# Layer 0 of a two-layer trunk: input and output projections as seven half-size products for eight, output projection behind all of y, norm first, Silu gate

## The chip, the core and the metric

The kernel runs on one core of a Trainium2 chip. The metric is the device time of one execution in microseconds (us), as the median of several runs. The engines are TensorE (PE, matmuls into PSUM), VectorE (DVE), ScalarE (ACT), GpSimd (POOL) and SyncE (SP, which here only issues DMAs). Each works through its own instructions in the order in which they stand in the program, and they wait for each other on semaphores.

## What is computed

Two layers on 1024 tokens of width 1024 in float32. Layer 0 is a pooling mixer, layer 1 stick-breaking attention; only layer 0 and the step into layer 1 matter here.

```python
D_MODEL, SEQ, D_INNER = 1024, 1024, 2048
POOL_WINDOWS = (2, 4, 8, 16)           # 4 groups of 512 channels

def causal_pool_minus_self(u, window): # trailing mean over min(t+1, window) positions, minus u[t]
    ...

def pooling_mixer(u, w_in, w_group, scale, w_out):
    proj = u @ w_in                    # (1024 x 1024) @ (1024 x 4096)
    xb, z = jnp.split(proj, 2, axis=-1)
    xg = xb.reshape(B, S, N_POOL_GROUPS, POOL_GROUP_DIM)
    pooled = jnp.stack(
        [causal_pool_minus_self(xg[:, :, gi], w) for gi, w in enumerate(POOL_WINDOWS)],
        axis=2)
    mixed = jnp.einsum('bsgi,gio->bsgo', pooled, w_group).reshape(B, S, D_INNER)
    y = mixed * scale * jax.nn.silu(z)
    return y @ w_out                   # (1024 x 2048) @ (2048 x 1024)

def reference(x, ...):
    h = x
    for i in range(DEPTH):             # layer 0: pooling_mixer, layer 1: attention
        u = rms_norm(h, norm_g[i])
        h = h + mixer(u)
    return rms_norm(h, norm_f)
```

## The kernel before

A float32 product is carried by three passes (`mm3`, L76 to L79): each operand is split into hi and lo parts, and hi·hi, hi·lo and lo·hi are accumulated in PSUM. A weight tile of 128x512 is split by an ACT copy (L91) and a DVE subtraction (L92). Nearly all matmuls of layer 0 have 128 rows and 512 columns. Tokens run in reversed order on the chip.

Layer 0 works on channels by rows and tokens by columns. x comes transposed from HBM (`xt`). The input is multiplied by the norm's gain (L162 on ACT, L163 on DVE for the remainder) but not by the norm's factor of a token: that factor, `rsb` on all partitions, is made beside the first products from a second copy of x (`load_h`, L99 to L103, L175, L176) and comes in on DVE when a projection leaves PSUM (`scaled`, L179). So the first matmul needs only one tile of x and one of weights.

A loop over the four windows then does, in each: four blocks of 128 channels of xb (`xb_block`: two halves of 512 tokens, each 8 contraction blocks times 3 passes, so 48 matmuls; doubling additions L204, a ratio L206, the subtraction L207, a split L209/L210); four blocks of gate (`gate`, 48 matmuls each, scaled, Sigmoid, product); and behind each gate block the group matrix on the pooled data (`mixed`, 24 matmuls, L223, and the split of y). Behind every second block the output projection of the two finished 128-row blocks of y is done at once (`late`, `out_proj`, L139 adds it onto h): 96 matmuls each time. The last of these are interleaved with the norm of layer 1 (`normed`) and 64 transposes of 128x128 (`transposed`, L114, L117, L118). In all, layer 0 has 1536 matmuls of input projection, 384 of group matrices and 768 of output projection.

The order on each engine is set by a scheduler that simulates the program; the loops above are the order in which it is written. POOL does little: memsets, the norm's small steps (L101, L103), and in layer 1 the masks (memset L433, selects L438 and L448, each 128x128), while DVE does scans with two SBUF inputs (L441).

Of the kernel before, what the change touches and what calls it, by code (L numbers as in the profile page):

```python
# [9 lines left out]
F32 = mybir.dt.float32  # L10
# [5 lines left out]
P = 128  # L16
# [3 lines left out]
NT = S // P          # token tiles  # L20
NK = D // P          # contraction blocks of the model width
# [15 lines left out]
def trunk(ctx, tc, x, xt, g, pw, pg, psc, pwo, sqk, sv, sz, swo, nf, out):  # L37
# [16 lines left out]
    ul = resid.tile([P, NK, S], F32R, name="ul")

# [4 lines left out]
    act(warm, warm, AF.Sigmoid)  # L60
# [4 lines left out]
    nc.gpsimd.memset(mhalf, -0.5)  # L65

    # Ratio of the full window to the window that the sequence start cuts off.
# [8 lines left out]
    def mm3(ps, lh, ll, rh, rl, start, stop):  # L76
        nc.tensor.matmul(ps, lhsT=lh, rhs=rh, start=start, stop=False)  # L77
        nc.tensor.matmul(ps, lhsT=lh, rhs=rl, start=False, stop=False)  # L78
        nc.tensor.matmul(ps, lhsT=ll, rhs=rh, start=False, stop=stop)  # L79

    def load_w(*srcs):
        """Load [128, n] blocks of weights and split them into (hi, lo) tiles of 512 columns."""
        tiles = []
        for src in srcs:
            n = src.shape[-1]
            raw = wraw.tile([P, D], F32, name="w_raw")
            nc.sync.dma_start(raw[:, :n], src)
            for c in range(0, n, 512):
                wh = wspl.tile([P, 512], F32R, name="w_hi")
                wl = wspl.tile([P, 512], F32R, name="w_lo")  # L90
                act(wh, raw[:, c:c + 512], AF.Copy)  # L91
                nc.vector.tensor_tensor(wl, raw[:, c:c + 512], wh, ALU.subtract)  # L92
                tiles.append((wh, wl))
        return tiles

    def rstd_of(t):
        ssq = small.tile([P, 1], F32, name="ssq")
        junk = small.tile([P, D], mybir.dt.bfloat16, name="junk", bufs=1)
        act(junk, h[:, t, :], AF.Square, accum_out=ssq)  # L99
        ms = small.tile([P, 1], F32, name="ms")  # L100
        nc.gpsimd.tensor_scalar(ms, ssq, 1.0 / D, EPS, ALU.mult, ALU.add)  # L101
# [4 lines left out]
    def normed(t, xt):  # L106
        rs = rstd_of(t)
        nc.vector.tensor_scalar_mul(xt, h[:, t, :], rs)

    def transposed(layer, half, xn):  # L110
        for k in range(NK):
            tp = ps_t.tile([P, 512], F32, name="pt")
            for j in range(4):
                nc.tensor.transpose(tp[:, j * P:(j + 1) * P], xn[j][:, k * P:(k + 1) * P], ident)  # L114
            gc = g_sb[:, layer * NK + k:layer * NK + k + 1]
            cs = slice(half * 512, half * 512 + 512)
            act(uh[:, k, cs], tp, AF.Copy, scale=gc)  # L117
            nc.vector.scalar_tensor_tensor(  # L118
                ul[:, k, cs], in0=tp, scalar=gc, in1=uh[:, k, cs], op0=ALU.mult, op1=ALU.subtract)

    def proj_ch(w2, half, pool=None):
        """[128 channels, 512 tokens] of u @ w for one block of 128 columns."""
        ps = pool.tile([P, 512], F32, name="pq") if pool else ps_d.tile([P, 512], F32, name="pd")
        cs = slice(half * 512, half * 512 + 512)
        for k in range(NK):
            wh, wl = w2[k // 4]
            ks = slice(k % 4 * P, k % 4 * P + P)
            mm3(ps, wh[:, ks], wl[:, ks], uh[:, k, cs], ul[:, k, cs], k == 0, k == NK - 1)
        return ps

    def out_proj(ys, w4, t):
        """h[t] += sum over two blocks of 128 rows; ys: (hi, lo) of [128, 128] each."""
        for n in range(2):
            po = ps_d.tile([P, 512], F32, name="pd")
            for i, (yh, yl) in enumerate(ys):
                wh, wl = w4[2 * i + n]
                mm3(po, yh, yl, wh, wl, i == 0, i == 1)
            cs = slice(n * 512, n * 512 + 512)
            nc.vector.tensor_tensor(h[:, t, cs], po, h[:, t, cs], ALU.add)  # L139

# [1 line left out]
    with tc.tile_pool(name="l0", bufs=2) as l0:  # L142
        def xn_tile(t):
            return l0.tile([P, S + 16], F32, name="xb" if t % 2 else "wsum")[:, :D]
# [3 lines left out]
        rsb = l0.tile([P, S], F32, name="rsb", bufs=1)  # L148
        xv = x.rearrange("(t p) c -> t p c", p=P)

        xs = {}

        def load_ut(half, ks, then=None):
            cs = slice(half * 512, half * 512 + 512)
            for k in ks:
                if k % 2 == 0:
                    xs["t"] = xn_tile(k // 2)
                xj = xs["t"][:, k % 2 * 512:k % 2 * 512 + 512]
                nc.sync.dma_start(xj, xt[k * P:(k + 1) * P, cs])
                if then:  # L160
                    then(k)
                act(uh[:, k, cs], xj, AF.Copy, scale=g_sb[:, k:k + 1])  # L162
                nc.vector.scalar_tensor_tensor(  # L163
                    ul[:, k, cs], in0=xj, scalar=g_sb[:, k:k + 1], in1=uh[:, k, cs],
                    op0=ALU.mult, op1=ALU.subtract)

        def load_h(half):
            for t in range(4 * half, 4 * half + 4):
                nc.sync.dma_start(h[:, t, :], xv[t])

        def factors(half):
            ps = ps_t.tile([P, 512], F32, name="pt")
            for j in range(4):
                rs = rstd_of(4 * half + j)
                nc.tensor.transpose(ps[:, j * P:(j + 1) * P], rs.broadcast_to([P, P]), ident)  # L175
            act(rsb[:, half * 512:half * 512 + 512], ps, AF.Copy)  # L176

        def scaled(dst, ps, half):
            nc.vector.tensor_tensor(dst, ps, rsb[:, half * 512:half * 512 + 512], ALU.mult)  # L179

        def gate(w2, half, t):
            ps = proj_ch(w2, half)
            scaled(t, ps, half)
            act(ps, t, AF.Sigmoid)
            nc.vector.tensor_tensor(t, ps, t, ALU.mult)

        def xb_block(gi, c, w2, pooled):
            w = WINDOWS[gi]
            xb = l0.tile([P, S + 16], F32, name="xb")
            nc.gpsimd.memset(xb[:, S:], 0.0)  # L190
            if gi == 0:
                pss = first[c]
            else:
                pss = [proj_ch(w2, half) for half in range(2)]
            if len(pss) < 2:
                pss.append(proj_ch(w_first[c], 1))
            for half in range(2):
                scaled(xb[:, half * 512:half * 512 + 512], pss[half], half)
# [12 lines left out]

        def mixed(gi, o, pooled, t0):
            kb = gi * 4 + o
            (gh, gl), = load_w(pg[kb])
            yh = l0.tile([P, S], F32R, name="y_h", bufs=4)
            yl = l0.tile([P, S], F32R, name="y_l", bufs=4)
            for half in range(2):
# [424 lines left out]
```

## Time and profile before

| | |
|---|---|
| median of 3 runs | 1613.57 us (1613.32 to 1613.58) |
| span of the profiled execution | 1613.1 us |
| PE busy | 99% |
| DVE / ACT / POOL busy | 65% / 37% / 10% |
| layer 0 ends, layer 1 begins | at about 640 us |

The profile gives each engine's busy time and, for groups of instructions, their count and mean duration. Matmuls are pipelined: one of 128x512 is listed with some 390 ns but the next begins after 0.23 us, so their pace is read from the count in a window and not from the mean. DVE instructions overlap a little too: "x2 | 1.30" is two instructions that begin one behind the other. A timeline's bracket gives the idle time before an instruction and what ended it.

### The profile page before, as it was taken

The numbers are of one execution on the slowest core, as the hardware profiler recorded it, in microseconds if no ns is written. First come the engines' busy times: TensorE is split into PE (matmuls) and PEld (weight loads), VectorE is DVE, ScalarE is ACT, GpSimd is POOL, SyncE is SP. The second block draws the span as 40 slices with busy tenths as digits, with TensorE's granted clock in tenths as the row PEclk, the third lists the DMA queues.
The fourth block names the chain that finished last, engine by engine and source line by source line (L and its number), as shares of the span: only waits on it lengthen the run. The fifth ranks groups of instructions, "written<-read, shape, count | busy, mean of one in ns | idle before, by whom it ended". The sixth has DMA issues, their size and how long they took to land.

```text
span 1613.1 us, 22462 instructions
## 1 busy us (share of the span) xinstructions
PE 1592.7 (99%) x8520; PEld 1365.5 (85%) x8520; DVE 1050.7 (65%) x1601; ACT 594.3 (37%) x1140; POOL 161.5 (10%) x673
## 2 busy tenths in 40 slices
PE   7999999999999999999999999999999999999997
PEld 6888888888888887888988988989989989989986
DVE  4745665565567557387767757757757757757678
ACT  6212121112112314355435335435335335435344
POOL 1000000000000001011101101102102102101112
PEclk9999999999999999999999999999999999999999
DMA  7102111111102110121021021021021021021012
GB/s 281 59 27 66 46 53 46 40 52 46 59 27 66 46 55 31 40 66 40 27 66 40 27 66 40 27 66 40 27 66 40 27 66 41 27 66 40 27 52 106
DMA packets 30139, 85.87 MB, mean 53 GB/s; under 512 B 4048, under 2 KB 4048, under 8 KB 30032
## 3 DMA queue, kind: packets, MB, share of 16 engines
q1 hardware_dynamic: 29888, 84.43, 16.4%
q8 instruction: 67, 1.10, 0.3%
q14 instruction: 40, 0.33, 0.1%
q10 hardware_dynamic: 144, 0.01, 0.0%
HBM read 71.84 MB, written 4.19 MB: 47 GB/s over the span
## 4 chain that ended last, share of the span: by engine, by line
PE 96%; DVE 2%; DMA 1%; ACT 0%; issue 0%; POOL 0%; SPq 0%; DVEq 0%; POOLq 0%; ACTq 0%
PE pd L77 27%; PE pd L78 27%; PE pd L79 27%; PE pt L473 4%; PE po L77 2%; PE po L79 2%; PE po L78 2%; PE pq L429 2%; PE pq L430 2%; DMA w_raw<-in_pw 0%; DVE h L139 0%; DVE om L441 0%; PE pt L114 0%; PE pq L77 0%; PE pq L79 0%; PE pq L78 0%
## 5 line engine op out<-in xcount | busy, mean ns | idle before, releaser
L77 PE MATMUL pd<-uh,w_hi 128*128 128x512 f32 x992 | 389.5, 393 | 0.7 <-DVE t L340 0.7
L78 PE MATMUL pd<-ul,w_hi 128*128 128x512 f32 x992 | 390.0, 393 | 0.1
L79 PE MATMUL pd<-uh,w_lo 128*128 128x512 f32 x992 | 385.8, 391 | 0.0
L91 ACT ACTIVATE w_hi<-w_raw 128x512 fp32r<-128x512 f32 x236 | 148.6, 631 | 368.1 <-PE pd L78 203.3
L441 DVE TENSOR_TENSOR_SCAN om<-om 128x257 f32<-128x257 f32 (+1 forms) x192 | 187.8, 979 | 84.6 <-POOL om L438 67.0
L92 DVE TENSOR_TENSOR w_lo<-w_raw,w_hi 128x512 fp32r<-128x512 f32 x236 | 161.6, 690 | 98.4 <-ACT w_hi L91 96.1
L77 PEld LDWEIGHTS pd<-uh,w_hi 128*128 128x128 f32 x992 | 186.8, 188 | 38.4 <-DVE t L340 1.1
L79 PEld LDWEIGHTS pd<-uh,w_lo 128*128 128x128 f32 x992 | 186.6, 188 | 38.1
L78 PEld LDWEIGHTS pd<-ul,w_hi 128*128 128x128 f32 x992 | 186.8, 188 | 37.7 <-DVE ul L118 0.9
L139 DVE TENSOR_TENSOR h<-pd,h 128x512 f32<-128x512 f32 x256 | 172.7, 686 | 64.0 <-PE pd L79 62.7
L77 PE MATMUL pd<-w_hi,y_h 128*128 128x512 f32 x512 | 205.5, 401 | 0.7 <-ACT y_h L502 0.4
L78 PE MATMUL pd<-w_lo,y_h 128*128 128x512 f32 x512 | 202.5, 395 | 0.0
L79 PE MATMUL pd<-w_hi,y_l 128*128 128x512 f32 x512 | 200.7, 394 | 0.0
L434 ACT ACTIVATE om<-pq 128x256 f32<-128x256 f32 (+1 forms) x192 | 94.4, 492 | 178.4 <-PE pq L430 171.0
L77 PE MATMUL pd<-w_hi,uh 128*128 128x256 f32 x512 | 146.6, 286 | 0.0
L78 PE MATMUL pd<-w_lo,uh 128*128 128x256 f32 x512 | 144.8, 283 | 0.0
L79 PE MATMUL pd<-w_hi,ul 128*128 128x256 f32 x512 | 144.7, 283 | 0.0
L79 PEld LDWEIGHTS pd<-w_hi,y_l 128*128 128x128 f32 x512 | 96.3, 188 | 21.3 <-DVE y_l L503 0.2
L477 DVE TENSOR_TENSOR at_l<-pt,at_h 128x512 fp32r<-128x512 f32 (+1 forms) x160 | 99.3, 627 | 21.9 <-ACT at_h L476 21.6
L77 PEld LDWEIGHTS pd<-w_hi,y_h 128*128 128x128 f32 x512 | 96.4, 188 | 20.0 <-DVE h L139 0.8
L78 PEld LDWEIGHTS pd<-w_lo,y_h 128*128 128x128 f32 x512 | 96.5, 189 | 18.8
L445 DVE TENSOR_TENSOR om<-pq,om 128x256 f32<-128x256 f32 (+1 forms) x192 | 105.4, 551 | 8.4
(99 smaller groups left out, 2393.1 us busy)
## 6 DMA issues: line engine op xcount, KB each, us to landing
w_raw<-in_pw SPq DMA_DIRECT2D x30, 512.0 KB, 3.3
w_raw<-in_pwo SPq DMA_DIRECT2D x16, 512.0 KB, 3.3
w_raw<-in_sqk SPq DMA_DIRECT2D x16, 512.0 KB, 3.3
w_raw<-in_sz SPq DMA_DIRECT2D x16, 512.0 KB, 3.3
w_raw<-in_sv SPq DMA_DIRECT2D x16, 512.0 KB, 3.3
w_raw<-in_swo SPq DMA_DIRECT2D x16, 512.0 KB, 3.3
h<-in_x SPq DMA_DIRECT2D x8, 512.0 KB, 6.9
w_raw<-in_pg SPq DMA_DIRECT2D x16, 256.0 KB, 2.7
```

The lines of the kernel that those rows point to most:

```text
L77: nc.tensor.matmul(ps, lhsT=lh, rhs=rh, start=start, stop=False)
L78: nc.tensor.matmul(ps, lhsT=lh, rhs=rl, start=False, stop=False)
L79: nc.tensor.matmul(ps, lhsT=ll, rhs=rh, start=False, stop=stop)
L91: act(wh, raw[:, c:c + 512], AF.Copy)
L92: nc.vector.tensor_tensor(wl, raw[:, c:c + 512], wh, ALU.subtract)
L139: nc.vector.tensor_tensor(h[:, t, cs], po, h[:, t, cs], ALU.add)
L429: nc.tensor.matmul(ps[:, :m], lhsT=ql, rhs=kh[:, k1 - m:k1], start=True, stop=False)
L434: act(om[:, 1:1 + n], pz, AF.Sigmoid, scale=-ZSCALE)
L441: nc.vector.tensor_tensor_scan(out=om[:, :1 + n], data0=om[:, :1 + n], data1=om[:, :1 + n], initial=1.0 if s.first else carry[r], op0=ALU. ...
L445: nc.vector.tensor_tensor(om[:, :n], pz, om[:, :n], ALU.mult)
L473: nc.tensor.transpose(tp[:, c * P:(c + 1) * P], om[:, (j - b0) * P:(j - b0 + 1) * P], ident)
L477: nc.vector.tensor_tensor(al[:, :n], tp[:, :n], ah[:, :n], ALU.subtract)
```

## The change

**Input projection.** The contraction (two halves of 512) and the tokens (two halves of 512) and pairs of 128-channel blocks make a 2x2 by 2x2 product, done with seven half-size products (Strassen, in Winograd's form). A pair of blocks costs 7 x 12 = 84 matmuls where it cost 96. The operands of x are seven sets of four tiles (`G[1]` to `G[7]`), made once: `to_u` (L173) scales a tile by gain and token factor, `u_sums` makes the sums, two of its four on DVE (L186, L189) and two on POOL (L188, L192), and `u_split` splits each. The sums of weights are made for every pair on POOL (L232, L233, L234, L257). The products' outputs are combined on DVE (`v`, `x_`, `out`) into xb or, with Silu on ACT, into the gate `t0`.

**Norm first.** Since x's sums need finished u, the column sums of squares come first: ACT squares the loaded tiles (L154), PE sums them with a matmul against ones (L156), then DVE, POOL, four transposes and an ACT copy make `rsb` (L160 to L167).

**Output projection behind all of y.** `mixed` stores each y block to HBM (`y_dram`, L297). After the last window the whole projection is done as seven products of 96 matmuls, in the order 1, 6, 2, 7, 4, 5, 3: y is loaded again in halves (L356), sums of y and of weights are made on POOL (40 additions for product 6: L404, L405, L406, L410, L411; 8 each for products 7, 4 and 3: L430, L434, L470; 8 onto h: L477, L483), and all of them are split as before. The norm of layer 1 and its transposes stand half between products 5 and 3 and half behind 3 (`to_u1`).

Layer 1 has the same work; its weight tiles are loaded in 512 columns at a time, and h is kept as 16 separate tiles.

```diff
-        load_ut(0, (0,), load_first)
-        load_ut(0, (1, 2, 3))
...
-        first = [[proj_ch(w_first[c], 0, ps_q if c < 2 else None)] for c in range(4)]
-        load_h(0)
-        factors(0)
-        load_ut(1, range(8))
...
+        def to_u(k, l, n, rsb):
+            j, kb = divmod(k, 4)
+            t = B[j, l, kb]
             nc.vector.scalar_tensor_tensor(
+                t, in0=t, scalar=g_sb[:, k:k + 1], in1=rsb, op0=ALU.mult, op1=ALU.mult)
+            if n:
+                u_split(n, kb, t)
...
+        def u_sums(kb):
+            b11, b21, b12, b22 = B[0, 0, kb], B[1, 0, kb], B[0, 1, kb], B[1, 1, kb]
+            t3 = l0.tile([P, 512], F32, name="w_raw", bufs=3)
+            nc.vector.tensor_tensor(t3, b22, b12, ALU.subtract)
+            u_split(7, kb, t3)
+            nc.gpsimd.tensor_tensor(b12, b11, b12, ALU.subtract)
+            nc.vector.tensor_tensor(b11, t3, b11, ALU.add)
+            u_split(6, kb, b11)
+            u_split(5, kb, b12)
+            nc.gpsimd.tensor_tensor(b11, b11, b21, ALU.subtract)
+            u_split(4, kb, b11)
...
+                add = nc.gpsimd.tensor_tensor
+                add(s1, a21, a22, ALU.add)
+                add(a21, a21, a11, ALU.add)
+                add(a11, a11, s1, ALU.add)
...
+        x0, x1 = Group(0), Group(2)
+        rsb = load_x(0, {1: x0.load, 3: x1.load})
+        for k in range(4):
+            to_u(k, 0, 1, rsb)
+        x0.first()
+        x1.first()
+        for k in range(4, 8):
+            to_u(k, 0, 2, rsb)
+        x0.second()
+        x1.second()
+        rsb = load_x(1)
+        for kb in range(4):
+            to_u(kb, 1, 0, rsb)
+            to_u(4 + kb, 1, 3, rsb)
+            u_sums(kb)
...
+            nc.sync.dma_start(y_dram[kb], t0)
...
+        def ops6(kb):
+            for jl in ((0, 1), (1, 1), (1, 0)):
+                load_y(*jl, kb)
+            T3[kb] = slot()
+            add(T3[kb], Y[1, 1, kb], Y[0, 1, kb], ALU.subtract)
+            add(Y[0, 1, kb], Y[0, 0, kb], Y[0, 1, kb], ALU.subtract)
+            add(Y[0, 0, kb], T3[kb], Y[0, 0, kb], ALU.add)
+            a21, a22, a11 = (wload(*ij, kb) for ij in ((1, 0), (1, 1), (0, 0)))
+            S1[kb] = ob.tile([P, 512], F32, name="s1", bufs=8)
+            S2[kb] = ob.tile([P, 512], F32, name="s2", bufs=8)
+            add(S1[kb], a21, a22, ALU.add)
+            add(S2[kb], S1[kb], a11, ALU.add)
+            return split(S2[kb]), split(Y[0, 0, kb], ob, "y")
```

Where the order moves. First PE at the start of the program. Before, `uh`/`ul` are the parts of x and `y_h`/`y_l` the parts of the first weights:

```order
L77 MATMUL pq_198<-uh_83,y_h_132 128x512
L78 MATMUL pq_198<-ul_84,y_h_132 128x512
L77 MATMUL pq_223<-uh_83,y_h_134 128x512
L78 MATMUL pq_223<-ul_84,y_h_134 128x512
L79 MATMUL pq_198<-uh_83,y_l_133 128x512
```

After, behind eight groups of column sums; `wsum`/`xb` hold squares, `rs4` the norm's factors, `g1` the first operand of x:

```order
L156 MATMUL bk_121<-ones_79,xb_184 128x2 x4
L165 MATMUL bk_194<-ident_72,rs4_192 128x128 x4
L88 MATMUL bk_221<-g1_0h_202,w_hi_222 128x512
L88 MATMUL bk_240<-g1_0h_202,w_hi_241 128x512
L156 MATMUL bk_315<-ones_79,wsum_318 128x2 x4
...
L156 MATMUL bk_315<-ones_79,wsum_366 128x2 x3
L156 MATMUL bk_315<-ones_79,xb_374 128x2 x4
L165 MATMUL bk_384<-ident_72,rs4_382 128x128 x4
L88 MATMUL bk_512<-g6_0h_405,w_hi_515 128x512
L89 MATMUL bk_512<-g6_0l_406,w_hi_515 128x512
```

The first products now stand behind the factors of one token half, and the sixth product (`g6`), after 48 matmuls, behind those of the other half.

POOL at the same place. Before, its rows of layer 0 are the norm's small steps and memsets:

```order
L190 MEMSET xb_430 128x16
L190 MEMSET xb_440 128x16
L101 TENSOR_SCALAR ms_398<-ssq_395 128x1
L103 TENSOR_TENSOR rs_400<-ms_398,mhalf_96 128x1
L101 TENSOR_SCALAR ms_406<-ssq_403 128x1
```

After, `pl` are tiles of u and `a_raw` loaded weights:

```order
L162 TENSOR_TENSOR rs4_382<-ms4_380,mhalf_77 128x4
L188 TENSOR_TENSOR pl_316<-pl_122,pl_316 128x512
L188 TENSOR_TENSOR pl_324<-pl_130,pl_324 128x512
L188 TENSOR_TENSOR pl_332<-pl_140,pl_332 128x512
L232 TENSOR_TENSOR w_raw_508<-a_raw_504,a_raw_506 128x512
L233 TENSOR_TENSOR a_raw_504<-a_raw_504,a_raw_132 128x512
L234 TENSOR_TENSOR a_raw_132<-a_raw_132,w_raw_508 128x512
L188 TENSOR_TENSOR pl_340<-pl_148,pl_340 128x512
L192 TENSOR_TENSOR pl_122<-pl_122,pl_158 128x512
```

Thirteen 128x512 additions now stand between the second factors and the last operand of the fourth product.

POOL where the output projection begins, after the last window; `slot` are halves of y, `w_raw` output weights, `s1` and `s2` their sums. Before, nothing stands there but the small steps of layer 1's norm:

```order
L190 MEMSET xb_3546 128x16
L101 TENSOR_SCALAR ms_4227<-ssq_4224 128x1
L103 TENSOR_TENSOR rs_4229<-ms_4227,mhalf_96 128x1
L101 TENSOR_SCALAR ms_4252<-ssq_4249 128x1
L103 TENSOR_TENSOR rs_4254<-ms_4252,mhalf_96 128x1
```

After:

```order
L404 TENSOR_TENSOR slot_3739<-slot_3735,slot_3733 128x512
L405 TENSOR_TENSOR slot_3733<-slot_3529,slot_3733 128x512
L410 TENSOR_TENSOR s1_3749<-w_raw_3743,w_raw_3745 128x512
L406 TENSOR_TENSOR slot_3529<-slot_3739,slot_3529 128x512
L411 TENSOR_TENSOR s2_3750<-s1_3749,w_raw_3747 128x512
L410 TENSOR_TENSOR s1_3789<-w_raw_3783,w_raw_3785 128x512
L404 TENSOR_TENSOR slot_3779<-slot_3775,slot_3773 128x512
L434 TENSOR_TENSOR slot_3529<-slot_3529,slot_3737 128x512
```

The row that writes the last `slot` operand of the sixth product is the 45th of such rows, five of them (L434) for the fourth product.

SP at that place, first before (output weights inside the windows), then after (`t0` is y of a block, stored ahead of the loads that follow):

```order
L87 DMA w_raw_4147<-in_pg 128x512
L87 DMA w_raw_4187<-in_pwo 128x1024
L87 DMA w_raw_4197<-in_pwo 128x1024
L87 DMA w_raw_4523<-in_sqk 128x1024
L87 DMA w_raw_4601<-in_sz 128x1024
```

```order
L297 DMA y_dram_114<-t0_3325 128x1024
L297 DMA y_dram_114<-t0_3326 128x1024
L356 DMA slot_3529<-y_dram_114 128x512
L103 DMA w_raw_3531<-in_pwo 128x512
L356 DMA slot_3553<-y_dram_114 128x512
L103 DMA w_raw_3555<-in_pwo 128x512
```

The loads of the first output product are issued only when the last block of y has been stored.

## Rows read from the trace of the kernel before

**Rows 1.** The page, parts 1 and 4: busy time by engine, chain of waits by engine

```profile
PE 1592.7 (99%) x8520; PEld 1365.5 (85%) x8520; DVE 1050.7 (65%) x1601; ACT 594.3 (37%) x1140; POOL 161.5 (10%) x673
PE 96%; DVE 2%; DMA 1%; ACT 0%; issue 0%; POOL 0%; SPq 0%; DVEq 0%; POOLq 0%; ACTq 0%
```

**Rows 2.** Windows of layer 0: window, length, then busy us and instructions by engine

```profile
200.00:400.00 200.00, 200.00 (x875) 163.99 (x874) 119.20 (x162) 43.53 (x67) 0.67 (x6) 1.00 0.15 49
400.00:600.00 200.00, 200.00 (x873) 163.73 (x872) 117.70 (x162) 39.52 (x61) 0.22 (x2) 1.00 0.15 49
```

**Rows 3.** Groups on POOL: form and count, busy us, mean ns, idle before

```profile
L448 POOL TENSOR_SCALAR_AFFINE_SELECT om<-om 128x128 f32<-128x128 f32 x128 | 55.2, 432 | 118.2 <-DVE om L445 118.1
...
L433 POOL MEMSET om<- 128x1 f32 x192 | 18.2, 98 | 305.2 <-DVE om L441 119.8 <-PE pt L473 87.6 <-DVE h L139 61.2
...
masks.py:199 POOL TENSOR_SCALAR_AFFINE_SELECT ident<-ident 128x128 f32<-128x128 f32 x1 | 0.3, 292 | 0.0
```

**Rows 4.** Timeline of POOL in layer 1: start us, duration us, instruction

```profile
993.48 0.29 POOL L438 TENSOR_SCALAR_AFFINE_SELECT om<-om 128x128 f32<-128x128 f32 x1 [1.11 <-ACT om L434]
...
995.05 0.82 POOL L448 TENSOR_SCALAR_AFFINE_SELECT om<-om 128x128 f32<-128x128 f32 x1 [0.84 <-DVE om L445]
...
997.56 0.62 POOL L448 TENSOR_SCALAR_AFFINE_SELECT om<-om 128x128 f32<-128x128 f32 x1 [1.54 <-DVE om L445]
```

**Rows 5.** Timeline of DVE over the same stretch

```profile
993.54 0.77 DVE L92 TENSOR_TENSOR w_lo<-w_raw,w_hi 128x512 fp32r<-128x512 f32 x1
...
994.84 0.94 DVE L441 TENSOR_TENSOR_SCAN om<-om 128x385 f32<-128x385 f32 x1
...
997.35 0.68 DVE L92 TENSOR_TENSOR w_lo<-w_raw,w_hi 128x512 fp32r<-128x512 f32 x1
```

**Rows 6.** Timeline of PE: first matmuls, and the first on pooled data

```profile
10.34 1.05 PE L77 MATMUL pq<-uh,y_h 128*128 128x512 f32 x2
11.20 0.48 PE L78 MATMUL pq<-ul,y_h 128*128 128x512 f32 x1
...
67.06 0.40 PE L77 MATMUL pd<-pooled,w_hi 128*128 128x512 f32 x1
```

**Rows 7.** DMA view of 0 to 30 us: GB/s moved, in 40 slices

```profile
GB/s 0 0 71 323 169 127 156 229 320 331 328 366 404 402 407 407 404 380 404 399 421 415 399 426 391 399 415 396 382 382 388 391 388 384 375 380 410 421 399 404
```

**Rows 8.** Timeline of ACT at the start

```profile
15.11 1.16 ACT L91 ACTIVATE w_hi<-w_raw 128x512 fp32r<-128x512 f32 x2 [0.55 <-DMA w_raw<-in_pw]
```

**Rows 9.** Timeline of DVE at the start

```profile
9.21 0.75 DVE L163 SCALAR_TENSOR_TENSOR ul<-wsum,g_sb,uh 128x512 fp32r<-128x512 f32 x1
9.88 1.42 DVE L163 SCALAR_TENSOR_TENSOR ul<-xb,g_sb,uh 128x512 fp32r<-128x512 f32 x2
...
15.77 1.30 DVE L92 TENSOR_TENSOR w_lo<-w_raw,w_hi 128x512 fp32r<-128x512 f32 x2 [0.43 <-ACT w_hi L91]
...
35.67 0.69 DVE L92 TENSOR_TENSOR w_lo<-w_raw,w_hi 128x512 fp32r<-128x512 f32 x1 [2.91 <-ACT w_hi L91]
```

**Rows 10.** Groups on DVE in 60 to 640 us, columns as in Rows 3

```profile
L223 DVE SCALAR_TENSOR_TENSOR t<-pd,sc_sb,t 128x512 f32<-128x512 f32 x32 | 23.9, 750 | 22.4 <-PE pd L79 22.4
...
L207 DVE SCALAR_TENSOR_TENSOR wsum<-wsum,xb 128x1024 f32<-128x1024 f32 x13 | 15.9, 1221 | 0.2
```

**Rows 11.** The page, part 6: loads of 256 KB, us from issue to landing

```profile
w_raw<-in_pg SPq DMA_DIRECT2D x16, 256.0 KB, 2.7
```

**Rows 12.** Windows at the end of layer 0, all instructions, then the transposes L114 alone

```profile
600.00:660.00 60.00, 57.17 (x265) 44.39 (x264) 37.90 (x56) 27.83 (x47) 6.83 (x24) 0.97 0.12 38
640.00:648.00 8.00, 6.91 (x25) 5.22 (x25) 3.29 (x5) 1.37 (x2) 0.00 (x0) 0.79 0.01 2
...
600.00:660.00 60.00, 10.71 (x64) 7.88 (x64) 0.97 0.12 38
```

More of the change, by code (lines that the diff above doesn't have):

```diff
@@ L59, in trunk @@
     nc.vector.memset(warm, 0.0)
-    act(warm, warm, AF.Sigmoid)
+    act(warm, warm, AF.Silu)
     sc_sb = const.tile([P, DI // P], F32, name="sc_sb")
@@ L73, in trunk @@
         ratio[w] = r
[L76 to L94, printed above, removed]
@@ new lines, in split, with raw_of, rstd_of @@
+    def split(raw, pool=None, name="w"):
+        pool = pool or wspl
+        hi = pool.tile([P, 512], F32R, name=f"{name}_hi")
+        lo = pool.tile([P, 512], F32R, name=f"{name}_lo")
+        act(hi, raw, AF.Copy)
+        nc.vector.tensor_tensor(lo, raw, hi, ALU.subtract)
+        return hi, lo
+    def raw_of(src, pool, name="w_raw", **kw):
+        raw = pool.tile([P, 512], F32, name=name, **kw)
+        nc.sync.dma_start(raw, src)
+        return raw
+    def rstd_of(parts):
+        n = len(parts)
+        ssq = small.tile([P, 2], F32, name="ssq")
+        for i, part in enumerate(parts):
+            junk = small.tile([P, 512], mybir.dt.bfloat16, name="junk", bufs=1)
+            act(junk, part, AF.Square, accum_out=ssq[:, i:i + 1])
+        if n == 2:
+            nc.gpsimd.tensor_tensor(ssq[:, 0:1], ssq[:, 0:1], ssq[:, 1:2], ALU.add)
@@ L121, in proj_ch @@
[L121 to L139, printed above, removed]
@@ L142, in trunk @@
[L142 to L187, printed above, removed]
-            w = WINDOWS[gi]
[L189 to L198, printed above, removed]
@@ L208, in xb_block @@
                 cur[:, :S], in0=cur[:, :S], scalar=1.0 / w, in1=xb[:, :S], op0=ALU.mult, op1=ALU.subtract)
-            act(pooled[0][:, c, :], cur[:, :S], AF.Copy)
-            nc.vector.tensor_tensor(pooled[1][:, c, :], cur[:, :S], pooled[0][:, c, :], ALU.subtract)
+            for half in range(2):
+                cs = slice(half * 512, half * 512 + 512)
+                hi, lo = pooled[c, half] = pl_tile(F32R), pl_tile(F32R)
+                act(hi, cur[:, cs], AF.Copy)
+                nc.vector.tensor_tensor(lo, cur[:, cs], hi, ALU.subtract)
@@ L257, in trunk @@
+        x0, x1 = Group(0), Group(2)
[9 more added lines that the diff above has]
+        rsb = load_x(1)
+        for kb in range(4):
+            to_u(kb, 1, 0, rsb)
+            to_u(4 + kb, 1, 3, rsb)
+            u_sums(kb)
         nc.sync.dma_start(sc_sb, psc)
-        load_h(1)
-        factors(1)
@@ L285, in trunk @@
-        w4 = load_w(pwo[14], pwo[15])
-        for half in (1, 0):
-            xn = []
-            for t in range(4 * half, 4 * half + 4):
-                out_proj(y_of(ys[-2:], t), w4, t)
-                xn.append(xn_tile(t))
-                normed(t, xn[-1])
-            transposed(1, half, xn)
-    with tc.tile_pool(name="l1", bufs=1) as l1:
+            pooled = {}
+            for cp in (0, 2):
+                grp = (x0 if cp == 0 else x1) if gi == 0 else Group(gi * 4 + cp)
+                if gi:
+                    grp.first()
+                dst = [xb_tile() for _ in range(2)]
+                grp.rest(dst, AF.Copy)
+                for i in range(2):
+                    pool_block(gi, cp + i, dst[i], pooled)
@@ new lines, in trunk, with slot @@
+            for op in (0, 2):
+                grp = Group(16 + gi * 4 + op)
+                grp.first()
+                dst = [l0.tile([P, S], F32, name="t0") for _ in range(2)]
+                grp.rest(dst, AF.Silu)
+                for i in range(2):
+                    mixed(gi, op + i, pooled, dst[i])
+    slots_ = ctx.enter_context(tc.tile_pool(name="slots", bufs=48, reuse_waits="tile"))
+    def slot(dtype=F32):
+        return slots_.tile([P, 512], dtype, name="slot")
+    h, u = {}, {}
@@ new lines, in trunk, with out_proj @@
+    ps_ctx.close()
+    act(warm, warm, AF.Sigmoid)
+    ps_d = ctx.enter_context(tc.tile_pool(name="ps_d", bufs=3, space=PSUM, reuse_waits="tile"))
+    ps_q = ctx.enter_context(tc.tile_pool(name="ps_q", bufs=2, space=PSUM, reuse_waits="tile"))
+    ps_t = ctx.enter_context(tc.tile_pool(name="ps_t", bufs=2, space=PSUM, reuse_waits="tile"))
+    ps_o = ctx.enter_context(tc.tile_pool(name="ps_o", bufs=1, space=PSUM, reuse_waits="tile"))
+    def out_proj(ys, w4, t):
+        for n in range(2):
+            po = ps_d.tile([P, 512], F32, name="pd")
+            for i, (yh, yl) in enumerate(ys):
+                wh, wl = w4[2 * i + n]
+                mm3(po, yh, yl, wh, wl, i == 0, i == 1)
+            nc.vector.tensor_tensor(h[t, n], po, h[t, n], ALU.add)
@@ L296, in trunk, with load_w @@
+    with tc.tile_pool(name="l1", bufs=1, reuse_waits="tile") as l1:
+        def load_w(*srcs):
+            return [split(raw_of(src[:, c:c + 512], l1, bufs=4))
+                    for src in srcs for c in range(0, src.shape[-1], 512)]
         NPAIR = NH // 2
@@ L391, in finish @@
             if not nfb:
[L392 to L394 removed]
+                for n in range(2):
+                    b = l1.tile([P, 512], F32, name="w_raw", bufs=4)
+                    nc.sync.dma_start(b, nf[:, n * 512:n * 512 + 512].broadcast_to([P, 512]))
+                    nfb.append(b)
             if t < LATE_T and not ended:
```

313 lines of the change are left out of this document (226 added, 87 removed).

## The prediction

> **What bounds the kernel now.** First the busy shares and the chain of waits [rows 1]: TensorE (PE) is busy 99% of the span and carries 96% of the chain, VectorE (DVE) 65%, GpSimd (POOL) 10%. What the reader is to see: nothing but PE time is on the path, so removed matmuls pay in full only while every operand is still ready in time. Then PE's pace in undisturbed layer 0 [rows 2]: 400 us hold 875 + 873 matmuls, 0.2289 us each. Then the start, the end of layer 0, and the engine that the change loads most, POOL.
>
> **Products removed: −65.9 us.** Before, layer 0 has 1536 matmuls of input projection, 384 with the group matrices and 768 of output projection. After, seven products for eight: 1344 + 384 + 672 = 2400. The 288 removed are worth 288 × 0.2289 = 65.9 us. The order of the changed kernel has these counts, so the change does what it says there; the question is what feeds them.
>
> **The price of one POOL addition, a.** The change puts on POOL 128x512 float32 additions of two SBUF tiles: 8 in the u sums, 4 for each of 16 groups, 64 for the output products and 8 for h. No row of before shows one, so I bound it. POOL's 128x128 select takes 292 ns undisturbed and its smallest memset 98 ns [rows 3]: (292 − 98)/128 = 1.52 ns an element for one read. One such pass over 512 columns is 0.87 us, the low end; were each operand a pass, 98 + 2 × 776 = 1.65, the high end. Counting two reads and a write against one read and a write gives 1.26. I take **a = 1.2**, near that middle and a little under it, because the select also compares. The Trainium skill, GPSIMD Engine Reference, section 3.1, has a 2048-element float32 add at 4497 ns, which by length would be an estimated 1.12 us here; with the sum below that is 1635. No run here shows it.
>
> **Does POOL stand still beside DVE?** The same select has a mean of 432 ns where it waits its turn late in the kernel [rows 3]. The timelines show why [rows 4, 5]: it takes 0.29 alone, but 0.82 from 995.05, when a DVE scan with two SBUF inputs runs from 994.84 to 995.78, and 0.62 from 997.56, beside the split L92 that ends at 998.03. Both times POOL ends 0.1 to 0.15 after DVE. The other way, the L92 at 993.54 takes 0.77 where the one at 997.35 takes 0.68: POOL had begun at 993.48. So I count a POOL addition and a DVE operation with two SBUF inputs as exclusive, save about 0.2 us (POOL's 98 ns fixed part and the 0.08 by which DVE's successive operations overlap). The Trainium skill, same page, section 1, says that POOL shares its SBUF interfaces with such DVE instructions; the trace agrees with its 0.82 and 0.62 for 0.29. Its section 4.1 speaks against the change: an elementwise add of two inputs belongs on VectorE.
>
> **Start: +44.5 us.** Before, the first matmul on pooled data is at 67.06 with five blocks of 48 in front of it [rows 6], so 67.06 − 240 × 0.229 = 12.1 us are lost. Norm first makes the operands of the first product wait for all column sums. Loads run at 400 GB/s [rows 7], 0.65 us for 256 KB, and ScalarE (ACT) starts on the 14th such unit at 15.1, two copies in 1.16 [rows 8]. In the new order ACT writes the first factors only behind the squares of the 16th load: 15.1 + 1.3 + 0.6 for a square (as a copy) + 0.6 for the copy = 17.6. DVE then scales eight tiles at 0.67 (1.42 for two, less 0.75 for one) = 5.4, and the first remainder, 0.61 (1.30 less 0.69), is there at 23.6 [rows 9]. 48 matmuls follow, 11.0 us, with some 12 at the 0.43 that the first ones of before show (11.20 − 10.34 for two) [rows 6], +2.4: 37.0. Behind them stand the last column sums, the power, four transposes and a copy: 2.4, so the second factors are ready at 39.4. Now DVE has 41 operations up to the last remainder of the fourth product: 8 × 0.67 + 33 × 0.61 = 25.5. Interlocked with them are 13 POOL additions, at 13 × (a − 0.2) = 13.0 if exclusive. That is 78, where PE has done 93 matmuls = 21.3. Lost: 56.6, so +44.5 against before; 31.5 without exclusion.
>
> **Middle of layer 0: +3, from 0 to 10.** Per window PE has 432 matmuls = 98.9 us. DVE has 60 operations at 0.61, 8 at 0.67 and four pooling blocks of two to five passes of 1.22 [rows 10], 52 to 67 us with the short ones, plus 16 additions: 71 to 86. PE covers it, except in the xb half of the 16-wide window (54 against 38.5), of which the gate's products take up most. The Silu gate drops a Sigmoid product and the scaling per block, on engines with slack: nothing.
>
> **Output products: +42.** They stand behind all of y. SyncE (SP) has the store of the last t0, which waits for its last DVE product, ahead of the first loads. 0.75 for that product [rows 10], 2.7 for a load [rows 11], a split of 1.2 and the issues: the first matmul comes about 6 us after the last one. The sixth product's additions need 16 loads of the first product and then three y tiles: 19 × 0.65 + 2.7 + issues, about 17 us after the stage's end. From there POOL has 45 additions until the last operand (40, and 5 for a later product mixed in); DVE's some 23 splits between them add 23 × 0.5 = 11.5 if exclusive. With the last split (0.8) and the last twelve matmuls (2.75) the sixth product ends at 17 + 45a + 11.5 + 3.6 = 32 + 45a, 86 for a = 1.2, against 192 × 0.229 = 44 for a PE that never waits: 45a − 12 = +42. Without exclusion 45a − 23.5 = +30.5. Later products need one addition for twelve matmuls (1.2 against 2.75): covered.
>
> **Into layer 1: +3, from −3 to 6.** Before, 600 to 660 us holds 265 PE records, 64 of them transposes: 201 × 0.229 = 46, so 14 us go to transposes, waits and the half clock (0.79 at 640 to 648) [rows 12]. After, half the transposes stand between the last two products and half behind the last, where the last additions (0.7), eight squares (4.8), the power and a scaling leave PE some 8 us idle; 3.5 + 8 + 3.5 + 2 at half clock = 17. Layer 1 keeps its matmuls: 0, give or take 2.
>
> **Sum.** −65.9 + (31.5 + 13a − 2.6) + 3 + (45a − 12) + 3 = 58a − 43. For a = 1.2: +26.6. The profiled execution's span is 1613.1, the median of the runs 1613.57, half a microsecond apart; I set the sum on the median: **1640**.
>
> **Rivals.**
> (1) The forecast: exclusive, a = 1.2. Its bounds, a = 0.87 and 1.65, give +7.5 and +53, so 1621 to 1666.
> (2) POOL runs beside DVE. Then −65.9 + 31.5 + 3 + 45a − 23.5 + 3 = 45a − 52: +2 for a = 1.2, **1616**, a tie. For it: a long addition may move between DVE's accesses where a short select could not; against it: both selects in the rows ended just behind DVE.
> (3) The faster side, one mechanism: the addition streams at the select's rate and is not held off in the output stage, where POOL's 45 additions are all that PE waits for. 45 × 0.87 − 52 = −13, **1601**. It decides below a = 1.16 without exclusion; with it, below 0.74, which is under the low bound. For it: one read sufficed for the select's rate; against it: the second operand.
> (4) Worse: a = 1.65, or waits in the middle of layer 0 too: **1666**.
>
> **How the numbers follow.** Forecast 0.60, (2) 0.15, (3) 0.15, (4) 0.10. About 0.2%, 3.2 us, is what a measurement of this kernel can tell from no change. Faster: all of (3), 0.06 of (2), 0.03 of the forecast's low edge = 0.24; same: 0.05 of (2), 0.03 of the forecast = 0.08; slower: the rest, 0.68. The range reaches to (3) with 3 us of its unknowns, 1598, and to the forecast's upper bound, 1666; the forecast's own range is 1621 to 1666.
>
> **What would show each step.** PE idle from about 37 to 63 us at the start, ended by DVE L181 or POOL L188, L192. POOL's 128x512 additions with a mean of 1.2 or more, longer beside DVE; DVE's L181 and L173 over 0.69 and 0.75 there. A stretch of some 60 us at the start of the output stage with PE busy about half, its waits ending in the splits of L406 and L411, and a clock under 1 in those slices. Wrong would be: PE full in that stretch (a well under 1.1), a POOL that overlaps DVE freely (its additions as long beside DVE as alone), PE idle under 30 us at the start, or long waits in the middle of layer 0, where I see slack.

## The result, and the profile after

The changed kernel takes **1659.9 us** (median of 4 runs, 1659.24 to 1660.44) against 1613.57 us: a ratio of **1.0283** with a 95% interval of 1.0269 to 1.0298, so 46 us slower. The forecast was slower by 26.6, 1640, with a range to 1666: the direction, the places and two of the three large terms were right, and the sum was 20 us too small.

The page of the changed kernel, parts 1, 2 and 4 (rows of before: [rows 1]):

```profile
span 1657.7 us, 23250 instructions
...
PE 1565.2 (94%) x8360; PEld 1349.1 (81%) x8360; DVE 1110.8 (67%) x1643; ACT 672.6 (41%) x1328; POOL 383.7 (23%) x822
...
PE   7399999999985999799999999999999999999997
...
POOL 0542222223029552111111101102102102101113
PEclk9599999999997999899999999999999999999999
...
PE 89%; DVE 3%; POOL 3%; DMA 2%; issue 1%; SPq 1%; ACT 1%; POOLq 0%; DVEq 0%; ACTq 0%
```

PE has less work than before (1565 busy us against 1593) and is idle in three places: the second slice, the slices 12 and 13, and the 17th. In two of them POOL's digit is 5 or 9, where before it was 0. The windows (window, length, busy us and instructions of PE, PEld, DVE, ACT and POOL, granted clock as a share, DMA share, GB/s) give them by time; [rows 2] answer to the fourth:

```profile
0.00:40.00 40.00, 30.98 (x136) 28.94 (x136) 13.20 (x22) 21.49 (x35) 2.82 (x37) 1.00 0.43 152
40.00:80.00 40.00, 11.91 (x56) 9.28 (x55) 28.01 (x31) 13.02 (x23) 20.90 (x14) 0.62 0.00 0
80.00:120.00 40.00, 35.39 (x141) 28.69 (x142) 31.96 (x44) 13.10 (x23) 21.13 (x14) 0.91 0.23 78
120.00:460.00 340.00, 340.00 (x1501) 281.53 (x1501) 228.41 (x300) 110.27 (x187) 77.05 (x62) 1.00 0.21 70
460.00:480.00 20.00, 12.18 (x46) 9.59 (x46) 7.95 (x12) 5.45 (x9) 0.00 (x0) 0.83 0.61 198
480.00:500.00 20.00, 20.00 (x90) 16.54 (x89) 10.66 (x12) 7.00 (x13) 13.56 (x10) 1.00 0.91 323
500.00:520.00 20.00, 7.72 (x23) 5.63 (x22) 4.73 (x5) 4.60 (x8) 20.00 (x15) 0.76 0.90 301
520.00:540.00 20.00, 13.04 (x33) 9.68 (x33) 5.06 (x5) 2.52 (x4) 20.00 (x16) 0.67 0.63 208
540.00:560.00 20.00, 16.94 (x66) 13.55 (x66) 14.65 (x16) 9.49 (x17) 14.69 (x10) 0.89 0.38 128
560.00:640.00 80.00, 80.00 (x355) 66.26 (x354) 67.91 (x83) 39.69 (x76) 42.27 (x36) 1.00 0.41 132
```

From 120 to 460 us PE never waits: the middle of layer 0 costs nothing. Its pace there is 340/1501 = 0.2265 us for a matmul against 0.2289 in [rows 2]. From 500 to 540 POOL is busy for all 40 us and PE for half.

The timelines give the stations of a run. They are used for all kernels below; "last of layer 0's windows" is the last matmul ahead of the output projection, and times are starts in us.

| kernel | first product | last of layer 0's windows | first output matmul | last output matmul | first of layer 1 | end |
|---|---|---|---|---|---|---|
| before | 6.2 | (interleaved) | (interleaved) | 630.5 | 631.1 | 1613.1 |
| changed | 24.1 | 467.3 | 475.5 | 667.0 | 683.8 | 1657.7 |

In the kernel before, the first matmul of layer 1 comes at 631.1, right behind the last of the output projection and between the transposes (`pt`); PE's last wait among these ends at 641.9:

```profile
630.49 0.40 PE L79 MATMUL pd<-w_hi,y_l 128*128 128x512 f32 x1
...
631.09 0.48 PE L77 MATMUL pd<-uh,w_hi 128*128 128x512 f32 x1
...
642.29 0.27 PE L114 MATMUL pt<-ident,xb 128*128 128x128 f32 x1
642.32 0.48 PE L78 MATMUL pd<-ul,w_hi 128*128 128x512 f32 x1
```

With 2400 matmuls at 0.2267 us and 64 transposes at about 0.108, layer 0 of the changed kernel is 551 us of PE work in 683.8: 133 us are lost (the column sums count as lost). Before, by 642.3 (a cut behind that wait), it was 2688 at a mean of 0.2293 (two paces, see the end), 40 of the 64 transposes and the first 22 matmuls of layer 1, 626 us: 16.6 lost, 12.1 of it at the start [rows 6]. So:

| | forecast | measured |
|---|---|---|
| products removed | −65.9 | −72.4 |
| start and windows (75.8 lost until 467.5, against 12.1) | +47.5 | +63.7 |
| output stage (8.0 to the first matmul, then 191.7 for 155.8 of work) | +42 | +43.9 |
| into layer 1 (13.0 lost behind the last output matmul, against 4.5) | +3 | +8.5 |
| layer 1 itself (974.0, against 973.2: the 970.8 left at 642.3, plus the 22 matmuls, less 24 transposes) | 0 | +0.8 |
| sum | +26.6 | +44.5 of 44.6 between the spans |

### The profile page after: what moved, and what is told of

Its sections match the earlier page's. It is cut to its first block, busy times and chain, and to the rows that moved or that the text cites. A ratio compares the mean times of both kernels' runs of the same rounds, so it can differ in the third digit from the quotient of the medians.

```text
span 1657.7 us, 23250 instructions
## 1 busy us (share of the span) xinstructions
PE 1565.2 (94%) x8360; PEld 1349.1 (81%) x8360; DVE 1110.8 (67%) x1643; ACT 672.6 (41%) x1328; POOL 383.7 (23%) x822
## 3 DMA queue, kind: packets, MB, share of 16 engines
q8 instruction: 66, 1.08, 0.3%
## 4 chain that ended last, share of the span: by engine, by line
PE 89%; DVE 3%; POOL 3%; DMA 2%; issue 1%; SPq 1%; ACT 1%; POOLq 0%; DVEq 0%; ACTq 0%
PE pd L88 14%; PE pd L90 14%; PE pd L89 14%; PE bk L88 10%; PE bk L89 10%; PE bk L90 10%; PE pt L686 4%; PE po L88 2%; PE po L89 2%; PE po L90 2%; PE pq L642 2%; PE pq L643 2%; DMA slot<-y_dram 2%; PE bk L156 1%; POOL slot L405 0%
## 5 line engine op out<-in xcount | busy, mean ns | idle before, releaser
L88 PE MATMUL pd<-slot,w_hi 128*128 128x512 f32 x512 | 202.2, 395 | 8.4 <-DVE slot L465 8.4
L89 PE MATMUL pd<-slot,w_hi 128*128 128x512 f32 x512 | 201.9, 394 | 0.0
L90 PE MATMUL pd<-slot,w_lo 128*128 128x512 f32 x512 | 200.3, 392 | 0.0
L88 PE MATMUL pd<-w_hi,slot 128*128 128x256 f32 x512 | 146.4, 286 | 0.0
L90 PE MATMUL pd<-w_hi,slot 128*128 128x256 f32 x512 | 144.7, 283 | 0.0
L89 PE MATMUL pd<-w_lo,slot 128*128 128x256 f32 x512 | 144.3, 282 | 0.0
L88 PE MATMUL bk<-w_hi,y_hi 128*128 128x512 f32 x224 | 92.3, 418 | 30.5 <-ACT y_hi L97 22.3
L88 PEld LDWEIGHTS pd<-slot,w_hi 128*128 128x128 f32 x512 | 96.8, 189 | 27.0 <-DVE slot L465 8.7
L90 PEld LDWEIGHTS pd<-slot,w_lo 128*128 128x128 f32 x512 | 96.6, 189 | 19.6
L89 PEld LDWEIGHTS pd<-slot,w_hi 128*128 128x128 f32 x512 | 96.6, 189 | 18.7
L88 PE MATMUL pd<-w_hi,y_h 128*128 128x512 f32 x256 | 107.0, 418 | 0.4 <-ACT y_h L715 0.4
L89 PE MATMUL pd<-w_lo,y_h 128*128 128x512 f32 x256 | 102.2, 399 | 0.0
L90 PE MATMUL pd<-w_hi,y_l 128*128 128x512 f32 x256 | 100.3, 395 | 0.0
```

## Experiments

Each kernel but the last was run once beside the kernel before (1612.5 to 1614.5 us).

**The output stage's additions on VectorE** (e1_out_dve).

```diff
-        add = nc.gpsimd.tensor_tensor
+        add = nc.vector.tensor_tensor
```

> The changed kernel with every addition of the output stage (72, the 45 ahead of the sixth product's last operand among them) on VectorE instead of GpSimd. If GpSimd's additions hold the sixth product (1.22 to 1.25 us each where it runs alone, about 1.7 beside a VectorE operation), VectorE needs 45 + 24 operations of 0.61 = 42 us there, and the product ends some 27 us earlier: 1633. If the loads are the limit in that stretch (its DMA share is 0.76), the product ends as before: 1655 to 1660.

1637.9 us, 22 less. GpSimd was what held the sixth product: from the first output matmul to the last PE is idle 8.5 us, where it was 22.7, and the stage takes 170.1 us instead of 191.5. Windows of this kernel, columns as above:

```profile
480.00:500.00 20.00, 20.00 (x90) 16.57 (x89) 16.84 (x28) 8.96 (x16) 0.00 (x0) 1.00 1.01 347
500.00:520.00 20.00, 14.38 (x54) 10.62 (x52) 18.90 (x32) 6.09 (x10) 0.00 (x0) 0.91 0.95 321
520.00:540.00 20.00, 17.12 (x70) 12.91 (x71) 18.97 (x32) 8.19 (x14) 0.00 (x0) 1.00 0.89 312
```

All of the 8.5 us are in the last two. DVE is busy 18.9 of 20 there and the DMA engines 0.9 to 1.0: with POOL out of the way these two are the next that can hold it. DVE takes up the sixth product's sums at 533.7 instead of 558.2, so 24.5 us earlier, where 27 were expected.

**The input stage's additions on VectorE** (e2_in_dve): L188, L192 and the four of each group.

> The changed kernel with the additions of the u sums and of the input weights on VectorE instead of GpSimd. If the two engines exclude each other there, an addition costs VectorE 0.61 in place of the 1.07 by which a GpSimd addition holds it up, 13 times ahead of the fourth product: about 6 us less, 1654. If GpSimd works beside VectorE, VectorE's own chain grows by 13 x 0.61: 8 us more, 1668. The windows behind have slack on VectorE in both cases.

1654.4 us, as expected from exclusive engines. A sum on DVE is worth more than one beside DVE. The gain at the start is 5.1 us (the windows' last matmul at 462.2); behind it an output stage of 197.3 us, 5.7 longer for a reason that no run shows, and a step into layer 1 that is 5.5 shorter (see the banks below) cancel.

**Squares summed before TensorE** (e3_acc).

```diff
-                act(sq, t, AF.Square)
-                for j in range(4):
-                    nc.tensor.matmul(
...
+                if k == 0:
+                    acc = tmp()
+                    act(acc, t, AF.Square)
+                else:
+                    act(sq, t, AF.Square)
+                    nc.vector.tensor_tensor(acc, acc, sq, ALU.add)
+            for j in range(4):
+                nc.tensor.matmul(
```

> The changed kernel with the squares of a token half summed on VectorE first, so that TensorE has 4 column sums for a half in place of 32. If the 0.21 us that each column sum takes on TensorE is what delays the factors (22.0 for the first, 51.0 for the second), the first come some 4 us and the second some 10 us earlier: 1650. If the loads, ScalarE's squares or the u sums set the start whatever the sums take, it stays at 1657 to 1660.

1652.9 us, 7.0 less: the transposes of the second factors start at 41.14 instead of 49.30. The last output matmul is 7.2 us earlier, so nearly all of the 8.2 comes through.

**The second output product ahead of the sixth** (e4_order).

```diff
+        out_product(pa, ops2, True)
         pb = [bank() for _ in range(4)]
         out_product(pb, ops6)
...
-        out_product(pa, lambda kb: (split(wload(0, 1, kb)), split(Y[1, 0, kb], ob, "y")), True)
```

> The changed kernel with the output products in the order 1, 2, 6, 7, 4, 5, 3: the second, which needs no addition, stands ahead of the sixth. If GpSimd's queue holds the sixth product, 22 us of TensorE's work now cover it: about 20 us less, 1640. If the loads hold it, the second product's 16 loads now stand ahead of it too (10 us), and about 10 us are won: 1650.

1652.8 us, 7.1 less, and a miss for both: from the first output matmul to the last it is 190.2 us against 191.5, so the order alone won 1.3. The other 5.5 come later, from the step into layer 1 (11.2 us instead of 16.7; see the banks below). On POOL's timeline the first addition now starts at 496.19, where it was 486.36, since the second product's 16 loads stand ahead, and more of the additions fall beside DVE's splits (1.7 us instead of 1.25): 24 of the first 45 take over 1.5 us, where it was 17. What the new cover gives, the loads and the exclusion take back: the sixth product's sums begin on DVE at 574.2, not 558.2, and PE is idle 23.0 us in the stage as against 22.7.

**Both halves ahead of the first product** (f1_start): `load_x(1)` directly behind `load_x(0)`, with the two input edits above.

```diff
         rsb = load_x(0, {1: x0.load, 3: x1.load})
+        rsb_ = load_x(1)
...
-        rsb = load_x(1)
+        rsb = rsb_
```

> The changed kernel with both token halves loaded, squared and summed before the first product, the squares of a half summed on VectorE, and the additions of the input stage on VectorE. If the start is VectorE's chain of operations behind the second factors, and these stood behind the first products on TensorE, VectorE now runs through from 18 us: some 72 operations of 0.61 to 0.67 end at about 63 instead of 92, about 25 us less: 1634. If only the cost of the sums and of the GpSimd additions counts, it is the two single edits together, 7.0 + 5.5: 1647.

1633.7 us. The last matmul of the windows starts at 444.6 instead of 467.3. PE is still idle at the start, but behind DVE alone, which is busy from 17 to 65 us but for one wait of 2.7. PE's sixth product, first at 74.42 in the changed kernel, now starts at:

```profile
60.04 0.79 PE L88 MATMUL bk<-g_0h,w_hi 128*128 128x512 f32 x1 [14.18 <-ACT w_hi L97]
```

**Output stage with VectorE's additions and the order 1, 2, 6** (f2_out).

> The changed kernel with the output stage's additions on VectorE and the output products in the order 1, 2, 6, 7, 4, 5, 3. If additions are what TensorE waits for, 88 VectorE operations (54 us) and 72 loads (47 us at 400 GB/s) now both fit beside 66 us of products, and the stage's stall of 34 us goes: 1628 to 1632. If loads hold the products whatever the order, no more is won than by the additions alone: 1638.

1628.6 us. The stage itself is 165.3 us (191.5); 5.5 of the gain are again the step into layer 1. With DVE's additions the order pays 4.8 (165.3 against 170.1), where on POOL it had paid 1.3.

**Both** (f3_both), and with two more edits (f4_more): stores from POOL's queue and a last product whose second half goes token tile by token tile.

> The two kernels before it in one: the start with both halves first, and the output stage with VectorE's additions and the second product ahead. The places are 400 us apart and do not share a wait, so the gains should add: about 1605, under the kernel before (1614). If they do not add, something else (the end of layer 0, the first window) is late next: 1615 or more.

> The kernel with both edits, and two more: y is stored from GpSimd's queue, so that SyncE's loads do not stand behind the last store, and the second half of the last output product goes through its four token tiles one after the other, so that the norm of layer 1 starts on the first while TensorE works on the others. If the 7.8 us at the stage's beginning are the queue and the 8 to 9 us before layer 1 are the norm's chain, about 10 us less than the kernel with both edits: 1595. If the loads wait for the tiles' memory rather than for the queue, only the 5 to 6 us of the end: 1600.

1613.7 and 1606.7 us. The first misses its 1605 by 9: the start gains 22.6 us, as before, and the stage 23.8, where it had gained 26.3 alone, but the step into layer 1 is 16.7 us again, where each of its two parts had had 11.2. The second is 7.0 us faster than the first, between the 10 of one theory and the 5 to 6 of the other, and misses both totals because the first had missed: the first output matmul comes 6.0 us behind the windows' last (8.5 without the edit) and the step is 13.6.

**Banks** (g1_banks). PSUM is handed out in banks, one for the output of a product. In the changed kernel layer 1 opens its PSUM pools over the banks of layer 0. In the kernels with 16.7 its first product starts within 0.1 us of the end of DVE's read of the last of the eight transposed tiles, in those with 11.2 it starts 0.14 to 0.15 behind the read of the fourth: whose bank it takes would explain both.

```diff
-    ps_d = ctx.enter_context(tc.tile_pool(name="ps_d", bufs=3, space=PSUM, reuse_waits="tile"))
-    ps_q = ctx.enter_context(tc.tile_pool(name="ps_q", bufs=2, space=PSUM, reuse_waits="tile"))
     ps_t = ctx.enter_context(tc.tile_pool(name="ps_t", bufs=2, space=PSUM, reuse_waits="tile"))
+    ps_d = ctx.enter_context(tc.tile_pool(name="ps_d", bufs=3, space=PSUM, reuse_waits="tile"))
+    ps_q = ctx.enter_context(tc.tile_pool(name="ps_q", bufs=2, space=PSUM, reuse_waits="tile"))
```

> The changed kernel with nothing altered but the order in which layer 1's PSUM pools are opened, so that its first product takes the bank of the second of the last eight transposed tiles; in the changed kernel it takes the bank of the eighth. If the 16.7 us between the last output matmul and the first of layer 1 (11.2 in four of the other runs) hold a wait for that bank's reader, it becomes 11.2 or less: 1654. If it is the norm's chain or the weights, nothing: 1660.

1655.0 us, 5 less by nothing but the order in which pools are opened. PE's timeline, of the changed kernel and then of this one:

```profile
667.04 0.39 PE L90 MATMUL bk<-w_hi,y_lo 128*128 128x512 f32 x1
...
683.77 0.80 PE L88 MATMUL pd<-slot,w_hi 128*128 128x512 f32 x1 [8.42 <-DVE slot L465]
```

```profile
677.93 0.80 PE L88 MATMUL pd<-slot,w_hi 128*128 128x512 f32 x1 [2.27 <-ACT w_hi L97]
```

The first waited for L465, DVE's read of the last transposed tile (from 682.97, 0.75 long), though it needs the other token half: in g1_banks the same product runs while four of these reads are still to come.

**Eight products for the output** (h1_plain): that part of the change undone, the rest as in the changed kernel.

```diff
+        def half_out(l, n):
+            ps = [bank() for _ in range(4)]
+            for j in range(2):
+                def ops(kb):
+                    if n == 0:
+                        load_y(j, l, kb)
+                    return split(wload(n, j, kb)), split(Y[j, l, kb], ob, "y")
+
+                out_product(ps, ops, j == 1)
...
+        half_out(0, 0)
+        half_out(0, 1)
+        half_out(1, 0)
+        to_u1(0)
+        half_out(1, 1)
+        to_u1(1)
```

> The changed kernel with the output projection undone to eight plain products (768 matmuls, no sums of y or weights, no additions on GpSimd), still behind all of y. If what the seven products cost there is GpSimd's queue, the stall of 34 us goes and 96 x 0.2267 = 21.8 us of products come back: 1648, and 5 less if layer 1's first bank falls on an early tile. If the stage waits for loads, the stall stays and the products come on top: 1670 or more.

1641.4 us: **with 96 matmuls more it is 18.5 us faster.** The stage takes 179.1 us instead of 191.5, and PE does not wait in it:

```profile
480.00:560.00 80.00, 80.00 (x354) 66.24 (x353) 41.58 (x66) 35.54 (x63) 0.00 (x0) 1.00 0.66 237
560.00:640.00 80.00, 80.00 (x370) 66.65 (x370) 49.38 (x81) 42.06 (x80) 5.59 (x12) 1.00 0.28 96
```

Seven products on the output stage pay only with their additions on DVE (170.1, 165.3) and lose 12 with them on POOL. The rest of the 18.5 is the bank (11.1 to layer 1).

**All edits** (g4_final), timed against the kernel before.

> All edits in one: both halves first with the squares summed on VectorE, all additions on VectorE, the first product of a gate pair ahead of the u sums, output products in the order 1, 2, 7, 6, 4, 5, 3 with two of the seventh's additions per block taken from the sixth's five, stores from GpSimd's queue, the last product's second half by token tile, and an early bank for layer 1. Against 1606.7 of the kernel with six of these: 6 us of stall in the sixth product, about 3 in the bank and 2.7 of products at the start: 1596. If VectorE's total and not its order holds the output stage, 1602.

1598.2 us (median of 4) against 1612.5: a ratio of **0.9916**, 0.9900 to 0.9933, so the idea does beat the kernel before by 14 us once its additions, its start and its first bank are put right. That is 0.9%, clear of the spread of its runs (1597.3 to 1600.2). What still waits, in windows:

```profile
440.00:560.00 120.00, 108.96 (x463) 88.30 (x462) 101.53 (x166) 53.70 (x92) 1.07 (x2) 0.97 0.79 271
0.00:80.00 80.00, 41.73 (x162) 33.47 (x163) 66.08 (x108) 42.09 (x69) 4.43 (x40) 0.89 0.31 108
```

Most of it is the start: PE works 42 of the first 80 us, DVE 66. The output stage takes 165.1 us, only 1.5 less than without the new place of the seventh product (166.6 in f4_more). Its four waits behind the first matmul, 5.3 us in all, fall between 516 and 543 and each ends with a DVE operation, and DVE is busy 58 of the 60 us from 500 to 560. So the second theory's reading fits, though the time lies between the two values and no run took DVE's load alone away.

## Why the prediction was right in its direction and 20 us short

**Products removed: mechanism right, 6.5 us more.** 288 matmuls are gone; those left are also faster, 0.2267 against a mean of 0.2293.

**The price of an addition and the exclusion: right.** I took a = 1.2 and exclusive engines. In the sixth product POOL's rows read (POOL, then DVE over the same stretch):

```profile
502.85 1.26 POOL L404 TENSOR_TENSOR slot<-slot 128x512 f32<-128x512 f32 x1
504.07 1.25 POOL L411 TENSOR_TENSOR s<-s,w_raw 128x512 f32<-128x512 f32 x1
505.29 1.26 POOL L410 TENSOR_TENSOR s<-w_raw 128x512 f32<-128x512 f32 x1
506.52 1.70 POOL L406 TENSOR_TENSOR slot<-slot 128x512 f32<-128x512 f32 x1
508.19 1.26 POOL L404 TENSOR_TENSOR slot<-slot 128x512 f32<-128x512 f32 x1
```

```profile
506.02 1.08 DVE L98 TENSOR_TENSOR w_lo<-s,w_hi 128x512 fp32r<-128x512 f32 x1 [4.27 <-ACT w_hi L97]
```

Alone an addition follows the next after 1.22 us. Where a split runs, the addition behind it has 1.70 and the split 1.08 instead of 0.69 (1.75 at the start). The pair takes 1.67 (506.52 to 508.19), against 1.2 − 0.2 + 0.61 = 1.61 in my sum. Rivals (2) and (3) fall: the engines do not overlap, and a is far from 0.87. The time came out near rival (4)'s 1666, but not by its mechanism: a is not 1.65, and the middle of layer 0 has no waits. The Trainium skill, GPSIMD Engine Reference, section 4.1, which puts such additions on VectorE, agrees with the 22 us that moving them gave.

**Output stage: right, 43.9 for 42.** The terms hold: POOL starts 19 us after the windows' end (17 forecast), its 45 additions take 63 us, to 549.6 (54 + 11.5 forecast), and DVE takes up the sixth product's sums at 558, 91 after the windows' last matmul (86 forecast). The wait that PE's rows name is ACT's or DVE's split; the queue behind it is POOL's. Of the 35.9 us lost behind the first output matmul only 22.7 are idle time; the rest are 61 matmuls at the half clock, one every 0.43 us, behind the waits (granted 0.76, 0.67 and 0.89 in the windows from 500 to 560).

**The start: wrong, +63.7 for +47.5, and the step that failed is the last column sums, priced at next to nothing (inside a 2.4 that also held the power, the transposes and a copy).** PE at the start:

```profile
17.61 1.85 PE L156 MATMUL bk<-ones,xb 128*128 128x2 f32 x8
20.83 1.11 PE L165 MATMUL bk<-ident,rs 128*128 128x128 f32 x4 [1.37 <-POOL rs L162]
...
24.07 0.80 PE L88 MATMUL bk<-g_0h,w_hi 128*128 128x512 f32 x1 [2.13 <-ACT g_0h L180]
```

```profile
49.30 1.03 PE L165 MATMUL bk<-ident,rs 128*128 128x128 f32 x4 [1.35 <-POOL rs L162]
74.42 0.80 PE L88 MATMUL bk<-g_0h,w_hi 128*128 128x512 f32 x1 [24.09 <-ACT w_hi L97]
```

A column sum has two records of 0.21 us although only two columns move: 64 records, some 13.7 us, for the first half. PE, not the loads, set the first factors (22.6 instead of 17.6): the half's last square ends on ACT at 14.3, but its last sum on PE at 19.5, and from there to the scaling the power, the transposes and the copy take 3.1 us, of which my 17.6 held only the copy. The first remainder is 5.0 late with them (28.6). The second half's sums take 10.6 us of PE's time among the first products, more than half of them ahead of these products' second pass and 7.0 us behind the first remainder, while the 48 matmuls take 13.3, as forecast (13.4). So DVE has the second factors at 51.0 instead of 39.4. The kernel before has no matmul with so few columns, and I should have bounded it from both sides as I did for POOL: its 128x128 transposes, 64 for 10.71 busy us [rows 12], would have warned. Undoing it (e3_acc) gave back 7.0. The next step held in sum: DVE's chain from the second factors to the last operand is 40.7 us, 38.5 forecast. The interlocked operations cost 11.3 us for 13.0; two waits of 4.2 in all, which I had not counted, make up the rest. Its first and last rows, and one that POOL holds up:

```profile
51.00 1.41 DVE L173 SCALAR_TENSOR_TENSOR pl<-pl,g_sb,rsb 128x512 f32<-128x512 f32 x2 [2.84 <-ACT rsb L167]
...
62.35 1.75 DVE L189 TENSOR_TENSOR pl<-w_raw,pl 128x512 f32<-128x512 f32 x1 [1.15 <-POOL pl L188]
...
90.67 1.08 DVE L181 TENSOR_TENSOR g_3l<-pl,g_3h 128x512 fp32r<-128x512 f32 x1 [3.06 <-ACT g_3h L180]
```

The second wait, 3.1 ahead of the last row, is POOL's order: its last sum of u stands behind an addition of weights that begins at 85.18, after 3.5 us of waiting for its load. The remaining 5 us of the start are a wait of 4.1 on PE at 93 us for a combination on DVE (L251), which stands behind that last row, and matmuls at the half clock behind it (granted 0.91 from 80 to 120). The 3 us that I had set for the middle were not needed.

**Into layer 1: 8.5 for 3.** The bank of PSUM, which I had not looked at, adds some 5.5 (16.7 against 11.2; g1_banks); the other 3.0 are the norm's chain, as forecast. Layer 1 itself is 0.8 longer, within the 2 that I allowed.

## What to carry to other kernels

Price the work that feeds the operands, not only the products saved: seven products for eight save 21.8 us of matmuls on this output stage, gave 14.0 at best (165.1 against 179.1), and lose to eight when 45 additions stand on an engine that here takes turns with VectorE. Before a sum goes to GpSimd "because it is idle", put the pair's time there (1.67 here for 0.69 + 1.25); it was cheaper to give VectorE the addition too. And a chain that makes operands before the first product costs its whole length: start it first, run it on one engine without handing over, and put nothing of the next half behind the products of the first.

## Not expected of the hardware

- A float32 matmul that moves two columns took 0.43 us (two records of 0.21) at the start and about 0.23 behind the first products (8 records from 46.92 us on begin within 0.9): few columns do not make it cheap.
- The wait for a PSUM bank crosses pools: the first matmul of layer 1 came 5.5 us later where it waited for a reader of the last tile from the pool closed before it.
- Matmuls of the input projection followed each other after 0.227 us in both kernels, those of group matrices and output projection after 0.232 before and 0.227 after, with the same shapes and a granted clock of 1.00. No run tells why; it is 6.5 us of the result.
